# First product of three more regions in quarters, with the measures moved: a 4096-cubed matmul with leaky ReLU on one core

## The chip, the cores and the metric

The kernel runs on one core of a Trainium2 chip. A core has TensorE (PE) for matmuls, which write to PSUM, four engines beside it (VectorE, DVE; ScalarE, ACT; GpSimd, POOL; SyncE, SP), and 16 DMA engines that serve queues issued from SP, ACT and POOL. Every engine runs its instructions in order and waits on semaphores where it needs another engine's result. The metric is the device time of one execution in microseconds (us). The kernel before took 1514.64 us, the median of three runs (1513.80 to 1515.65).

## What is computed

```python
def setup_inputs():
    m, k, n = 4096, 4096, 4096
    return {"a": np.random.randn(m, k).astype(np.float32),
            "b": np.random.randn(k, n).astype(np.float32),
            "alpha": np.float32(0.01)}

def reference(a, b, alpha):
    x = np.matmul(a, b)
    return np.where(x > 0, x, alpha * x)
```

## The kernel before

**Tiling.** The output is cut into regions of 1024 x 1024, named (g, j): g is one of four groups of rows of A, j one of four pairs of column blocks of B. Region (0, 0) is computed first by its own code. Then one loop (`for i, (g, j) in enumerate(regions)`) goes over (0,1) (0,2) (0,3), then (1,2) (1,0) (1,3) (1,1), then (2,2) (2,0) (2,3) (2,1), then (3,2) (3,0) (3,1) (3,3). The inputs are rounded to 16 bits.

**Seven products.** A region is one step of Strassen's method in Winograd's form: A's group and B's pair are 2 x 2 blocks (of 512 x 2048 and 2048 x 512), and seven products of such blocks, numbered 0 to 6 in the code, make the region: a11 b11, a12 b21, s2 T2, s3 T3, s1 T1, a22 T4, s4 b22. The sums s1 to s4 of A are made once for a group; the sums of B are made in place in each region by VectorE (`b_sum`, L583): T3 = b22 - b12 in b12's tile, T2 = T3 + b11 in b11's tile, T4 = b21 - T2 in b21's, and T1 = b22 - T2 in b11's again. B's tiles come in two parts, k = 0 and 1 (in the later groups, part 1 first). A full product (`product`, L906) is 64 matmuls of 512 columns.

**Quarters.** Many products take a second step of the same method: seven quarter products (`quarter_product`, L750) of 16 matmuls of 256 columns, 112 half-width matmuls in place of what would be 128. They need sums of quarters of A's block and of B's block (called t(1) to t(4) for B), again from VectorE (L674 to L697), and copies or additions between banks. Group 0 has none of them in this loop. In most regions of the later groups products 3 to 6 are in quarters; in a region that turns to the next group (the last of its group, (1,1) and (2,1)) only product 3 is, in `fourth_in_quarters`, whose third quarter product uses t(4), made on L682 after t(2) on L680.

**The first product in quarters.** In the regions of the set `FIRST` (before: (2,0), (2,3), (3,0), (3,1), (3,3)) product 0 is in quarters too: `for_the_first` (L1126 to L1140) makes seven sums on VectorE during the seventh product of the region before, and `first_in_quarters` makes one more (L1157) and two additions in PSUM (L1164, L1166), with the copies L1153 to L1170 on ScalarE. The other full products of such a region run as 128 half-width matmuls (L887), since its banks hold quarters.

**Measures.** To judge at the end whether 16 bits were enough, the kernel sums squares of all blocks of A and B (`Measure`, L224 to L268): four squares by ScalarE (L233) into rooms of a 4 KB-per-partition tile, then additions, a fold and a reduction on VectorE (L242 to L267). `EARLY` lists which block a region measures ahead of or behind its T sums, `IN_C` the region that puts the squares in c's tiles. If the judgement fails, a slow path of plain matmuls runs instead; with this input it does not.

**Tiles and queues.** There are three tiles `a16` (rooms for squares, for quarters' sums and for pieces of the next group's A), two times two tiles `c0` and `c1` (results before they are stored; the regions take them in turn, `side`), three large tiles `x`, of which two hold s1 and s4 while the third is s2 in the first half of a region and the quarters' room after it, and two tiles for each of b11, b12, b21, b22. b's blocks come as 32-bit data through POOL's queue, which converts them (L541), or as 16-bit copies kept in DRAM (`kept`, `kept_half`, `kept_t`) through SP's queue (L536 to L538). SP also stores results (L1235) and loads s2 (L769) and kept sums. In a region that turns, which (0,3) does too, pieces of the next group's A come through POOL (L134) into `a16`, VectorE transposes them (L143) and ScalarE squares them (L600); a new piece is fetched when both have let go of an old one's tile.

**Order.** The program's order is written by hand and kept (`manual_schedule`): each engine executes its instructions in the order of the code. The steps that the prediction follows: in (0,3) T sums, transposes of four pieces, T4, four more, T1; in (1,1) and (2,1) a measure, the T sums, one transposed piece, a part of T4, t3 of b12, two pieces, a store's leaky ReLU, one piece, the other part of T4, t(2), t(4), t(1).

Of the kernel before, what the change touches and what calls it, by code (L numbers as in the profile page):

```python
# [36 lines left out]
LAST = 1  # L37
OTHERS = (0, 3)
KEPT_T = {CACHED: 1, 0: 2, 3: 2}

# [7 lines left out]
def kernel(  # L50
# [474 lines left out]
    def fetch_unit(i, u, nt, later=False):  # L525

        g, j = regions[i]
        half = u // 2
        t = b_pool.tile([P, KC, NT], DT, name="b", tag=f"b{half + 1}{nt + 1}")
        have_b[i, u, nt] = t  # L530
        if later:
            nc.vector.memset(t[:, :1, :1], 0.0)
        if g > KEPT_T.get(j, G) and (half, nt) == (0, 1):
            move_t("t3", j, t, u, False)
        elif g and j == CACHED:
            nc.sync.dma_start(t, rows_of(kept[nt], u, 0, KC, True))  # L536
        elif half and (g and j == LAST or g > 1 and j in OTHERS):
            nc.sync.dma_start(t.rearrange("p c n -> p (c n)"), kept_half[j][u - 2, nt])  # L538
        else:
            for c in range(0, KC, 4):  # L540
                nc.gpsimd.dma_start(t[:, c:c + 4, :], b_rows(j, u, c, 4, nt, g > 0))  # L541
            if j == CACHED:
                wide = KC // (RUNS + [1, 1])[u]
                for c in range(0, KC, wide):
                    nc.sync.dma_start(rows_of(kept[nt], u, c, wide, False), t[:, c:c + wide, :])
# [39 lines left out]
    def measure(i, which, x, y):  # L585

        if which:
            tiles = [have_b[i, 2 * x + k, y] for k in ((1, 0) if regions[i][0] else (0, 1))]
        else:
            tiles = [at[regions[i][0], x, 2 * y + k] for k in range(2)]  # L590
        parts = halves(tiles[0]) + halves(tiles[1])
        return Measure(which, parts, not which)
# [15 lines left out]
    def judge(line):  # L608
# [26 lines left out]
    A11, A12, A22 = (0, 0, 0), (0, 0, 1), (0, 1, 1)  # L635
    B11, B12, B21, B22 = ((1, half, nt) for half in range(2) for nt in range(2))
    EARLY = {
        (1, 0): [B21], (1, 3): [B11], (1, 1): [B11], (2, 3): [B21], (2, 1): [B12], (3, 1): [B21],
    }
    IN_C = (3, 0)  # L640
    MEASURED = {
        (0, 1): (None, [B22], B12, B11), (0, 2): (B21, [B22, A22, A11], B12, A12),
        (3, 3): (B22, [], None, None),
# [7 lines left out]
    kept_s2 = dram_pool.tile([2, P, KC * RM], DT, name="kept_s2")  # L651
    kept_q = {name: dram_pool.tile([4, P, QUARTER], DT, name=f"kept_q{name}") for name in ("a22", "s4", "s1")}
    made = dram_pool.tile([2, NT], DT, name="made")
    FIRST = {(2, 0), (2, 3), (3, 0), (3, 1), (3, 3)}
    kept_s3 = dram_pool.tile([P, QUARTER], DT, name="kept_s3")
    kept_x21 = {name: dram_pool.tile([P, QUARTER], DT, name=f"kept_x{name}") for name in ("a22", "s4")}
    side = 0
# [203 lines left out]
    for i, (g, j) in enumerate(regions):  # L861
# [10 lines left out]
        else:  # L872
            Y, Z = Z, Y

        def keep_half(some=(0, 1)):
            for nt in some:
                for k in ks:
                    nc.sync.dma_start(kept_half[j][k, nt], B(1, nt, k).rearrange("p c n -> p (c n)"))

        def product(n, banks, first):  # L880
# [401 lines left out]
        early = [measure(i, *block) for block in EARLY.get((g, j), [])]  # L1282
        have_t2 = g > KEPT_T.get(j, G)
        at_once, afterwards = ([], early) if in_first or have_t2 else (early[:1], early[1:])
        for m in at_once:
            m.begin()
        if first_of_group and g:
            keep_s2(g)
        if in_first:
            shared = new_bank(shared_bank)  # L1290
            first_in_quarters(y, shared, z, first_t, first_s)
            new_s(g, "s2")
            load_s2(g, ks[0])
        else:
            product(0, y, True)
        if second_of_group:
            sums_of_s3(g, (2,))
        for m in at_once:
# [4 lines left out]
        if have_t2:  # L1303
            for k in ks:
                t = have_b[i, k, 0] = b_pool.tile([P, KC, NT], DT, name="b", tag="b11")
                move_t("t2", j, t, k, False, nc.scalar)
        in_c = (g, j) == IN_C
        if in_c:
            m = measure(i, *B22)
            m.room = [c_pool.tile([P, 2048], BF16, name="sq", tag=f"c{n}") for n in (side, side, 1 - side, 1 - side)]  # L1310
            for n in range(4):
                m.square(n)
        if second_of_group:
            in_other = lambda n: c_pool.tile([P, QUARTER], DT, name="sums", tag=f"c{1 - side}") if n == 4 else new_a16()
            sums_of_a(g, "s1", in_other if g == 1 else new_a16, m.end if in_c else None)
# [19 lines left out]
            middle.end()  # L1335
        if i == 0:
            first_measure.end()
        for m in [] if have_t2 else afterwards:
            m.end()
        if final:  # L1340
            judged = judge(a16_pool.tile([1, P * 6], FP32, name="line", tag="a16"))
# [1 line left out]
        if (g, j) == (0, LAST):  # L1343
            for k in ks:
                nc.sync.dma_start(made[k:k + 1], B(0, 0, k)[:1, 0, :])
        if g == 1 and j in OTHERS or (g, j) == (0, LAST):
            keep_half((0,))
        note_rows()
        if first_of_group:
            sum_a(g, "s3")  # L1350
# [18 lines left out]
            b_sum(B(1, 0, ks[0]), B(1, 0, ks[0]), B(0, 0, ks[0]), SUB)  # L1369
        if final:  # L1370
            good = next(judged)
        if (g, j) == (0, LAST):
            keep_half((1,))
        for k in [] if in_fourth else ks[1:] if turning and g else ks:
            b_sum(B(1, 0, k), B(1, 0, k), B(0, 0, k), SUB)
# [15 lines left out]
        if in_fourth:  # L1391
            s5[3] = t[:, 3]
            load_sums("s1", s5, (3,))
            if g == 1 and j in OTHERS:
                keep_half((1,))
        if turning and g:
            tq, sx4 = {2: t[:, 0], 4: t[:, 1], 1: t[:, 2]}, t[:, 3]
            sums_of_b(quarters_of_b(i, 0, 1), tq, (2, 4, 1))
# [71 lines left out]
        elif turning and g:  # L1470
            v_pairs, v, parts = fourth_in_quarters(z, tq, {**s3_rooms(g), 4: a_quarter(sx4)})
            if turning:
                for n in range(3):
                    turn_a_in(0, 1, n)
            for n, (to, bank) in enumerate(parts):
                nc.vector.tensor_add(to, bank, to)
            if turning:
                add_v()
            if turning:
                z = [new_bank(Z[mt]) for mt in range(MT)]  # L1480
                for mt in range(MT):
                    nc.scalar.copy(z[mt], u2[mt])
        else:
            product(3, z, True)
            v_pairs, v = keep(z, side)
        if in_quarters and first_of_group:
            tq = {2: t[:, 0], 1: t[:, 1], 4: t[:, 2]}
        fetch_b(i + 1, [(0, 1)], (1, 0) if in_fourth else (0, 1) if turning and g else ks)
        if turning:
            new_s(g + 1, "s2")  # L1490
            if g:
                bring_a(0, 1, [3])
            note_rows(1)
            for n in range(3):
                fetch_a(1, 0, n)
            turn_a_in(1, 0, 0)
            fetch_a(1, 0, 3)
            load_x21(g, "a22")
            load_x21(g, "s4")
# [12 lines left out]
        if in_quarters:  # L1512
            banks = [new_bank(Z[n]) for n in range(MT)]
            tq, sq = sixth_in_quarters(u2_pairs, banks, v_pairs, v, y, tq, sq)
        else:
            add(v, y)
            leave(v_pairs, 1, 1)
        if turning:
            for n in range(1, MT):
# [9 lines left out]
        if not in_quarters:  # L1529
            product(5, z, False)  # L1530
            if g:
                for mt in range(MT):
                    nc.scalar.copy(u2[mt], z[mt])
            else:
                add(u2[::-1], z[::-1])
        if turning:
# [18 lines left out]
        if in_quarters:  # L1555
# [4 lines left out]
            if final:  # L1560
                even, last = seventh_at_the_end(*rest, new_bank(Z[1]), new_bank(Z[0]))
            else:
                first_t, first_s = {}, {}
                between = for_the_first(tq, sq, first_t, first_s) if next_first else nothing()
                kept_c = seventh_in_quarters(*rest, between)
                fetch_b(i + 1, [(1, 1)], (1, 0))
                if not next_first:
                    new_s(g, "s2")
                    load_s2(g, 1)
                leave(kept_c, 0, 1)  # L1570
# [83 lines left out]
```

## Time and profile before

| | |
|---|---|
| runs | 1514.64 us (median of 3) |
| profiled execution, its own time | 1514.02 us |
| span of the profile (first to last instruction) | 1512.2 us |
| TensorE busy | 1503.5 us, 99% of the span |
| VectorE busy | 1212.0 us, 80% |
| ScalarE busy | 527.7 us, 35% |
| DMA | 384.99 MB, 255 GB/s on the mean |
| region (0,3) | 312.31 to 409.00 us |
| region (1,3) | 592.87 to 683.37 us |
| region (1,1) | 683.37 to 778.47 us |
| region (2,1) | starts at 1050.39 us |

The profile is one execution, taken by the hardware profiler. Its span leaves out 1.8 us around the first and last instruction. In a row of the timeline stand start, length, engine, line of the code, operation, the tiles written and read, their shapes and the count of merged instructions; in brackets the idle time before it and what ended it. "SPq" and "ACTq" are issues of DMAs. The end of a matmul is modelled, so its drawn length overlaps the next one's start.

### The profile page before, as it was taken

To read this page: it belongs to the slowest core of one execution; us is meant where nothing else is said; L and a number is where in the kernel's file an instruction comes from. 1 tells how busy PE (TensorE), PEld (TensorE's weight loads), DVE (VectorE), ACT (ScalarE), POOL (GpSimd) and SP (SyncE) were. 2 spreads that over 40 slices of the span, in tenths; PEclk is the share of its full clock that TensorE was granted. 3 is DMA by queue.
4 is the path that set the end of the run, shared out by engine and by line. 5 is a ranking of instruction groups with operands and counts; after the bars stand their busy time and mean duration, and the time that the engine had idled before them with its cause. 6 is when DMAs were issued, how large, how long until landed. Compare 5 with 4: busy or idle time off the path is not lost.

```text
span 1512.2 us, 24641 instructions
## 1 busy us (share of the span) xinstructions
PE 1503.5 (99%) x9979; PEld 975.2 (64%) x9979; DVE 1212.0 (80%) x1259; ACT 527.7 (35%) x911; POOL 252.3 (17%) x418
## 2 busy tenths in 40 slices
PE   9999999999999999999999999999999999999998
PEld 4465444444446577584544788888554488888887
DVE  4599867786796797788779698987887878998797
ACT  2402535657410323126561122323574113242322
POOL 4641110233202011013220101000331000100000
PEclk9999999999999999999999999999999999999999
DMA  9999895999889999999898989979989697987845
GB/s 239 188 191 246 236 284 176 161 204 192 217 351 229 291 304 293 299 285 277 205 252 329 285 314 249 354 232 325 243 206 295 264 278 279 251 291 185 349 153 183
DMA packets 193970, 384.99 MB, mean 255 GB/s; under 512 B 17587, under 2 KB 126389, under 8 KB 178742
## 3 DMA queue, kind: packets, MB, share of 16 engines
q0 software_dynamic: 115584, 108.03, 45.0%
q1 hardware_dynamic: 71062, 245.53, 43.5%
q10 hardware_dynamic: 7200, 29.76, 5.0%
q8 instruction: 80, 1.31, 0.3%
q14 instruction: 44, 0.36, 0.1%
HBM read 359.66 MB, written 129.50 MB: 323 GB/s over the span
## 4 chain that ended last, share of the span: by engine, by line
PE 98%; DVE 1%; issue 0%; ACT 0%; DVEq 0%; ACTq 0%
PE ps L906 49%; PE ps L750 34%; PE ps L887 9%; PE ps L275 5%; PE wp L107 0%; DVE c L305 0%; DVE a L369 0%; DVE c L1188 0%; ACT a L369 0%; PE turned L362 0%; DVE q L1133 0%; DVE q L1132 0%; DVE q L1126 0%; DVE q L1137 0%; DVE a L733 0%
## 5 line engine op out<-in xcount | busy, mean ns | idle before, releaser
L906 PE MATMUL ps<-b,a 128*128 128x512 f16 x1984 | 431.6, 379 | 0.0
L906 PEld LDWEIGHTS <-a 128*128 128x128 f16 x1984 | 194.1, 98 | 233.0
L906 PE MATMUL ps<-b,s 128*128 128x512 f16 x1472 | 321.5, 379 | 0.0
L906 PEld LDWEIGHTS <-s 128*128 128x128 f16 x1472 | 144.0, 98 | 173.4 <-issue 0.2
L750 PEld LDWEIGHTS <-q 128*128 128x128 f16 x2192 | 214.1, 98 | 26.1 <-issue 0.7
L541 POOL DMA_DIRECT2D b<-in_b_dram x120 | 89.0, 746 | 848.2 <-PE ps L906 303.2
L583 DVE TENSOR_TENSOR b<-b 128x4096 f16<-128x4096 f16 x82 | 185.8, 2285 | 39.5 <-DMA b<-in_b_dram 30.4
L143 DVE STREAM_TRANSPOSE a<-a 128x512 uint32<-128x512 uint32 (+2 forms) x120 | 126.9, 1105 | 65.2 <-DMA a<-in_a_dram 65.2
L134 POOL DMA_DIRECT2D a<-in_a_dram x252 | 137.4, 553 | 249.8 <-ACT junk L600 82.2
L929 ACT COPY c<-ps 128x512 f32<-128x512 f32 x164 | 86.2, 595 | 262.8 <-PE ps L906 179.5
L750 PEld LDWEIGHTS <-a 128*128 128x128 f16 x1536 | 150.3, 98 | 18.7
L305 DVE SCALAR_TENSOR_TENSOR c<-c 128x1024 f32<-128x1024 f32 (+2 forms) x123 | 141.8, 1191 | 5.9 <-ACT c L929 5.6
L600 ACT ACTIVATE junk<-a 128x512 bf16<-128x512 f16 x192 | 121.2, 631 | 71.8 <-DMA a<-in_a_dram 49.8
L233 ACT ACTIVATE sq<-b 128x2048 bf16<-128x2048 f16 x60 | 111.4, 1910 | 62.9 <-DVE sq L242 54.7
L750 PE MATMUL ps<-b,q 128*128 128x256 f16 x1088 | 128.1, 273 | 0.0
L750 PE MATMUL ps<-q,q 128*128 128x256 f16 x1024 | 119.0, 273 | 0.0
L750 PE MATMUL ps<-b,a 128*128 128x256 f16 x976 | 114.5, 273 | 0.0
L750 PEld LDWEIGHTS <-s 128*128 128x128 f16 x960 | 93.9, 98 | 11.4
L275 PE MATMUL ps<-b,a 128*128 128x512 f16 x384 | 84.5, 379 | 1.8 <-DVE a L369 0.7
L887 PE MATMUL ps<-b,a 128*128 128x256 f16 x640 | 70.7, 273 | 0.0
L887 PE MATMUL ps<-b,s 128*128 128x256 f16 x640 | 70.7, 273 | 0.0
L934 DVE TENSOR_TENSOR c<-ps,c 128x512 f32<-128x512 f32 x76 | 47.0, 680 | 29.3 <-PE ps L906 29.3
(166 smaller groups left out, 1393.9 us busy)
## 6 DMA issues: line engine op xcount, KB each, us to landing
b<-in_b_dram POOLq DMA_DIRECT2D x128, 512.0 KB, 12.7
out_dram<-c SPq DMA_DIRECT2D x118, 512.0 KB, 8.2
a<-in_a_dram POOLq DMA_DIRECT2D x244, 128.0 KB, 5.6
b<-kept_half SPq DMA_DIRECT2D x28, 1024.0 KB, 11.9
b<-kept SPq DMA_DIRECT2D x20, 1024.0 KB, 9.4
q<-kept_qs ACTq DMA_DIRECT2D x40, 512.0 KB, 7.8
s<-kept_s SPq DMA_DIRECT2D x18, 1024.0 KB, 7.4
q<-kept_qs SPq DMA_DIRECT2D x28, 512.0 KB, 5.9
```

The costliest lines, as they stand in the source:

```text
L134: nc.gpsimd.dma_start(a16[32 * q:32 * q + 32], src.rearrange("(g i) w -> i g w", i=32))
L143: nc.vector.transpose(part.rearrange("p c m e -> p c (m e)").bitcast(U32) .rearrange("p c (g i) -> p g c i", i=32), src[:, :, i * n:(i + 1 ...
L233: nc.scalar.activation(to, self.parts[n], SQUARE)
L275: nc.tensor.matmul(ps, a_cols(at[0, h, u], c, mt), bt[0, u, nt][:, c, :], start=first, stop=last,)
L305: nc.vector.scalar_tensor_tensor(t, t, alpha, t, op0=MULT, op1=MAX if alpha <= 1 else MIN)
L541: nc.gpsimd.dma_start(t[:, c:c + 4, :], b_rows(j, u, c, 4, nt, g > 0))
L583: nc.vector.tensor_tensor(f(to), f(x0), f(x1), op)
L600: nc.scalar.activation(junk, piece[:, q, :], SQUARE, accum_out=to[:, 4 * n + q:4 * n + q + 1])
L750: nc.tensor.matmul(to[m], xq[:, c // 2, rows, c % 2], yq[:, c, :], start=first and c == 0 and m < banks, stop=c == KC - 1, skip_group_chec ...
L887: nc.tensor.matmul(to, a_cols(operand(g, name, k), c, q // 2 * 2 + m), B(half, nt, k)[:, c, q % 2 * HALF:(q % 2 + 1) * HALF], start=False, ...
L906: nc.tensor.matmul(banks[mt], a_cols(t, c, mt), B(half, nt, k)[:, c, :], start=first and (k, c) == todo[0], stop=(k, c) == todo[-1], skip_ ...
L929: nc.scalar.copy(to, bank)
```

## The change

- `FIRST` gains (1,3), (1,1) and (2,1): their product 0 is in quarters, their other full products in half-width matmuls. Lines that assumed whole banks now go by `pieces` (copies of z, of u2, and the addition of y).
- The measure of b11 in (1,3) goes to (0,3) (in both regions it is pair 3's b11), with its squares in c's tiles and one a16; it stays ahead of the T sums there. The measures of (1,1) (b11) and (2,1) (b12) put their four squares in c's tiles, behind the first product's copies, and their VectorE part comes behind the T sums.
- b22 of pair 3 is stored in 16 bits in (0,3) (`KEPT_IN`, `keep_half`), after b12 of the next region is fetched, and no longer in (1,3); (1,3) loads it from there on SP's queue. In place of standing behind the seventh product of (1,0), this load stands behind the first half of s2 in (1,3) (`LATE`).

Counted in the built program: SP issues 2 stores of 1 MB more in (0,3), 2 stores fewer and 2 loads more in (1,3), and POOL 4 loads of 512 KB fewer for (1,3). ScalarE's and VectorE's lists change only in the regions named.

```diff
--- before.py
+++ after.py
@@ -37,6 +37,8 @@
 LAST = 1
 OTHERS = (0, 3)
 KEPT_T = {CACHED: 1, 0: 2, 3: 2}
+KEPT_IN = {(LAST, 0): 0, (LAST, 1): 0, (0, 0): 1, (0, 1): 1, (3, 0): 1, (3, 1): 0}
+LATE = (1, 3)
 
 
 
@@ -534,7 +536,7 @@
             move_t("t3", j, t, u, False)
         elif g and j == CACHED:
             nc.sync.dma_start(t, rows_of(kept[nt], u, 0, KC, True))
-        elif half and (g and j == LAST or g > 1 and j in OTHERS):
+        elif half and g > KEPT_IN.get((j, nt), G):
             nc.sync.dma_start(t.rearrange("p c n -> p (c n)"), kept_half[j][u - 2, nt])
         else:
             for c in range(0, KC, 4):
@@ -635,9 +637,9 @@
     A11, A12, A22 = (0, 0, 0), (0, 0, 1), (0, 1, 1)
     B11, B12, B21, B22 = ((1, half, nt) for half in range(2) for nt in range(2))
     EARLY = {
-        (1, 0): [B21], (1, 3): [B11], (1, 1): [B11], (2, 3): [B21], (2, 1): [B12], (3, 1): [B21],
+        (0, 3): [B11], (1, 0): [B21], (2, 3): [B21], (3, 1): [B21],
     }
-    IN_C = (3, 0)
+    IN_C = {(1, 1): B11, (2, 1): B12, (3, 0): B22}
     MEASURED = {
         (0, 1): (None, [B22], B12, B11), (0, 2): (B21, [B22, A22, A11], B12, A12),
         (3, 3): (B22, [], None, None),
@@ -651,7 +653,7 @@
     kept_s2 = dram_pool.tile([2, P, KC * RM], DT, name="kept_s2")
     kept_q = {name: dram_pool.tile([4, P, QUARTER], DT, name=f"kept_q{name}") for name in ("a22", "s4", "s1")}
     made = dram_pool.tile([2, NT], DT, name="made")
-    FIRST = {(2, 0), (2, 3), (3, 0), (3, 1), (3, 3)}
+    FIRST = {LATE, (1, 1), (2, 0), (2, 3), (2, 1), (3, 0), (3, 1), (3, 3)}
     kept_s3 = dram_pool.tile([P, QUARTER], DT, name="kept_s3")
     kept_x21 = {name: dram_pool.tile([P, QUARTER], DT, name=f"kept_x{name}") for name in ("a22", "s4")}
     side = 0
@@ -872,9 +874,9 @@
         else:
             Y, Z = Z, Y
 
-        def keep_half(some=(0, 1)):
+        def keep_half(some):
             for nt in some:
-                for k in ks:
+                for k in ks if KEPT_IN.get((j, nt)) == g else ():
                     nc.sync.dma_start(kept_half[j][k, nt], B(1, nt, k).rearrange("p c n -> p (c n)"))
 
         def product(n, banks, first):
@@ -1282,6 +1284,9 @@
         early = [measure(i, *block) for block in EARLY.get((g, j), [])]
         have_t2 = g > KEPT_T.get(j, G)
         at_once, afterwards = ([], early) if in_first or have_t2 else (early[:1], early[1:])
+        if at_once and not g:
+            in_c = [c_pool.tile([P, 2048], BF16, name="sq", tag=f"c{side}") for _ in range(2)]
+            at_once[0].room = [*in_c, a16_pool.tile([P, 2048], BF16, name="sq", tag="a16"), in_c[1]]
         for m in at_once:
             m.begin()
         if first_of_group and g:
@@ -1293,6 +1298,8 @@
             load_s2(g, ks[0])
         else:
             product(0, y, True)
+        if (g, j) == LATE:
+            fetch_b(i, [(1, 1)], ks)
         if second_of_group:
             sums_of_s3(g, (2,))
         for m in at_once:
@@ -1304,12 +1311,15 @@
             for k in ks:
                 t = have_b[i, k, 0] = b_pool.tile([P, KC, NT], DT, name="b", tag="b11")
                 move_t("t2", j, t, k, False, nc.scalar)
-        in_c = (g, j) == IN_C
+        in_c = IN_C.get((g, j))
+        after_t2 = []
         if in_c:
-            m = measure(i, *B22)
+            m = measure(i, *in_c)
             m.room = [c_pool.tile([P, 2048], BF16, name="sq", tag=f"c{n}") for n in (side, side, 1 - side, 1 - side)]
             for n in range(4):
                 m.square(n)
+            if turning:
+                after_t2.append(m)
         if second_of_group:
             in_other = lambda n: c_pool.tile([P, QUARTER], DT, name="sums", tag=f"c{1 - side}") if n == 4 else new_a16()
             sums_of_a(g, "s1", in_other if g == 1 else new_a16, m.end if in_c else None)
@@ -1335,7 +1345,7 @@
             middle.end()
         if i == 0:
             first_measure.end()
-        for m in [] if have_t2 else afterwards:
+        for m in after_t2 if have_t2 else afterwards + after_t2:
             m.end()
         if final:
             judged = judge(a16_pool.tile([1, P * 6], FP32, name="line", tag="a16"))
@@ -1343,8 +1353,7 @@
         if (g, j) == (0, LAST):
             for k in ks:
                 nc.sync.dma_start(made[k:k + 1], B(0, 0, k)[:1, 0, :])
-        if g == 1 and j in OTHERS or (g, j) == (0, LAST):
-            keep_half((0,))
+        keep_half((0,))
         note_rows()
         if first_of_group:
             sum_a(g, "s3")
@@ -1369,7 +1378,7 @@
             b_sum(B(1, 0, ks[0]), B(1, 0, ks[0]), B(0, 0, ks[0]), SUB)
         if final:
             good = next(judged)
-        if (g, j) == (0, LAST):
+        if i == 0:
             keep_half((1,))
         for k in [] if in_fourth else ks[1:] if turning and g else ks:
             b_sum(B(1, 0, k), B(1, 0, k), B(0, 0, k), SUB)
@@ -1391,8 +1400,7 @@
         if in_fourth:
             s5[3] = t[:, 3]
             load_sums("s1", s5, (3,))
-            if g == 1 and j in OTHERS:
-                keep_half((1,))
+            keep_half((1,))
         if turning and g:
             tq, sx4 = {2: t[:, 0], 4: t[:, 1], 1: t[:, 2]}, t[:, 3]
             sums_of_b(quarters_of_b(i, 0, 1), tq, (2, 4, 1))
@@ -1478,14 +1486,16 @@
                 add_v()
             if turning:
                 z = [new_bank(Z[mt]) for mt in range(MT)]
-                for mt in range(MT):
-                    nc.scalar.copy(z[mt], u2[mt])
+                for to, bank in pieces(u2_pairs, z):
+                    nc.scalar.copy(bank, to)
         else:
             product(3, z, True)
             v_pairs, v = keep(z, side)
         if in_quarters and first_of_group:
             tq = {2: t[:, 0], 1: t[:, 1], 4: t[:, 2]}
         fetch_b(i + 1, [(0, 1)], (1, 0) if in_fourth else (0, 1) if turning and g else ks)
+        if not g and i:
+            keep_half((1,))
         if turning:
             new_s(g + 1, "s2")
             if g:
@@ -1513,7 +1523,7 @@
             banks = [new_bank(Z[n]) for n in range(MT)]
             tq, sq = sixth_in_quarters(u2_pairs, banks, v_pairs, v, y, tq, sq)
         else:
-            add(v, y)
+            add_pieces(v_pairs, y)
             leave(v_pairs, 1, 1)
         if turning:
             for n in range(1, MT):
@@ -1529,8 +1539,8 @@
         if not in_quarters:
             product(5, z, False)
             if g:
-                for mt in range(MT):
-                    nc.scalar.copy(u2[mt], z[mt])
+                for to, bank in pieces(u2_pairs, z):
+                    nc.scalar.copy(to, bank)
             else:
                 add(u2[::-1], z[::-1])
         if turning:
@@ -1563,7 +1573,8 @@
                 first_t, first_s = {}, {}
                 between = for_the_first(tq, sq, first_t, first_s) if next_first else nothing()
                 kept_c = seventh_in_quarters(*rest, between)
-                fetch_b(i + 1, [(1, 1)], (1, 0))
+                if regions[i + 1] != LATE:
+                    fetch_b(i + 1, [(1, 1)], (1, 0))
                 if not next_first:
                     new_s(g, "s2")
                     load_s2(g, 1)
```

## The prediction

> **What bounds the kernel now.** I read the page first (busy time, chain of waits), then what TensorE waited for, then the timelines of TensorE, VectorE, ScalarE and the issue queues around the changed regions. From the page:
>
> ```profile
> PE 1503.5 (99%) x9979; PEld 975.2 (64%) x9979; DVE 1212.0 (80%) x1259; ACT 527.7 (35%) x911; POOL 252.3 (17%) x418
> PE 98%; DVE 1%; issue 0%; ACT 0%; DVEq 0%; ACTq 0%
> ```
>
> Matmuls set the end. TensorE's longest wait after the first stage is this one, from the view of who waited for whom:
>
> ```profile
> PE ps L750 <- ACT ps L1153: 0.4, 1, 0.4
> ```
>
> So there is no stall to remove: a change gains only by shorter matmul work, and any lateness that it puts on VectorE, which is 80% busy, is paid in full once it is past that engine's slack. TensorE's timeline, in (0,3), then (1,3) and (1,1), then (2,3), which already starts in quarters (columns: start, length, group):
>
> ```profile
> 353.75 13.98 PE L906 MATMUL ps<-b,a 128*128 128x512 f16 x64
> 367.56 13.98 PE L906 MATMUL ps<-b,s 128*128 128x512 f16 x64
> ...
> 592.87 27.79 PE L906 MATMUL ps<-b,a 128*128 128x512 f16 x128
> 620.62 13.97 PE L906 MATMUL ps<-b,s 128*128 128x512 f16 x64
> ...
> 724.81 3.66 PE L750 MATMUL ps<-b,a 128*128 128x256 f16 x32
> 728.30 1.91 PE L750 MATMUL ps<-q,a 128*128 128x256 f16 x16
> ...
> 961.25 1.91 PE L750 MATMUL ps<-b,a 128*128 128x256 f16 x16
> 973.54 14.14 PE L887 MATMUL ps<-b,a 128*128 128x256 f16 x128
> 987.51 14.14 PE L887 MATMUL ps<-b,s 128*128 128x256 f16 x128
> ```
>
> Starts are what counts, since the drawn lengths overlap. A full product takes 367.56 - 353.75 = 13.81 us. The first product in quarters takes 973.54 - 961.25 = 12.29, its short wait for L1153 included. A product in half-width matmuls, which such a region uses for its other full products, takes 987.51 - 973.54 = 13.97.
>
> **The gain: TensorE's work.** Each of (1,3), (1,1), (2,1) saves 13.81 - 12.29 = 1.52 on its first product and pays 0.16 for each product that goes to half-width: products 1 and 2 in (1,3), products 1, 2, 4, 5 and 6 in the regions that turn to the next group, (1,1) and (2,1). That is -1.52 + 0.32 = -1.20, and twice -1.52 + 0.80 = -0.72: together **-2.64 us**. Everything else can only cost.
>
> **(1,1) and (2,1): VectorE reaches the fourth product late.** Let F be the start of a region's first product. The second product after it now starts at F + 12.29 + 13.97 = F + 26.26 and ends at F + 40.23; the fourth product's third quarter needs the sum t(4) at 728.30 - 724.81 = 3.49 after that, F + 43.72. Before, in (1,1), VectorE did this:
>
> ```profile
> 705.72 2.10 DVE L143 STREAM_TRANSPOSE a<-a 128x512 uint32<-128x512 uint32 x2
> ...
> 719.55 2.25 DVE L583 TENSOR_TENSOR b<-b 128x4096 f16<-128x4096 f16 x1
> 725.01 1.23 DVE L680 TENSOR_TENSOR q<-b 128x2048 f16<-128x2048 f16 x1 [3.21 <-PE ps L906]
> 726.27 1.23 DVE L682 TENSOR_TENSOR q<-b,q 128x2048 f16<-128x2048 f16 x1
> 727.41 1.22 DVE L684 TENSOR_TENSOR q<-b,q 128x2048 f16<-128x2048 f16 x1
> ```
>
> From the first transpose (705.72) to the last b21 sum (721.80) it works without a pause, 16.1 us, then idles 3.21 and makes t(2) and t(4) in 727.41 - 725.01 = 2.4: ready at 727.4, 0.9 before use. So the slack is 3.2 + 0.9. What comes ahead of that block now is read from (2,3), VectorE first, then ScalarE:
>
> ```profile
> 972.60 2.28 DVE L583 TENSOR_TENSOR b<-b 128x4096 f16<-128x4096 f16 x1
> 974.83 0.06 DVE L768 MEMSET s<- 128x1 f16 x1
> 974.91 6.82 DVE L583 TENSOR_TENSOR b<-b 128x4096 f16<-128x4096 f16 x3
> 981.65 1.22 DVE L242 TENSOR_TENSOR sq<-sq 128x2048 bf16<-128x2048 bf16 x1
> ...
> 984.85 1.22 DVE L246 TENSOR_TENSOR sq<-sq 128x2048 bf16<-128x2048 bf16 x1 [0.65 <-ACT sq L233]
> ...
> 988.82 2.35 DVE L305 SCALAR_TENSOR_TENSOR c<-c 128x1024 f32<-128x1024 f32 x2
> ...
> 974.27 5.51 ACT L233 ACTIVATE sq<-b 128x2048 bf16<-128x2048 f16 x3
> ```
>
> The T sums cannot start before F + 11.35 (972.60 - 961.25), since VectorE first serves the quarters. In (1,1) the measured block is B11, which T2 overwrites, so T2's first half waits for two squares. ScalarE starts them after its bank copies at F + 13.02 and spaces them 1.80: the second is done at F + 16.7, the fourth at F + 20.3. T2, T3, T2 then take 6.82: F + 23.6. The measure takes 988.82 - 981.65 less its wait, 6.5: F + 30.1. The block of 16.1 and the 2.4 follow: t(4) is there at F + 48.6, **4.9 us late**. In (2,1) the block is B12, which T3 overwrites, so all four T sums (9.1) stand behind F + 16.8: 2.3 later still, **7.2 us late**. Lower bound for both, if no square were waited for: T sums from F + 11.35, t(4) at F + 45.4, 1.7 late. Upper bound: 1 more, if a square waits for c's tile to be stored. Queued behind are T1, the transposes and the fourth product's additions; T1 is next, 4.5 us after t(1), and the fourth product's five remaining quarters cover it.
>
> **(0,3): the measure of (1,3)'s old place.** Its squares use c's two tiles that the region before has just stored. Issue and landing of those stores (the tile's view in that window):
>
> ```profile
> L1235 SPq DMA_DIRECT2D out_dram<-c x2: 372/372/373, 308.1 to 309.2; - x2
> DMA to landing us min/median/max: 8.9/9.6/10.3
> ```
>
> So the first square starts at 317.0 to 318.4, and the fourth, which reuses the second's tile, ends at 324.4 to 325.9. VectorE adds it in and folds in 988.82 - 984.85 = 4.0: 328.4 to 329.9. VectorE and the queue of A's fetches (POOL) before:
>
> ```profile
> 318.86 4.69 DVE L583 TENSOR_TENSOR b<-b 128x4096 f16<-128x4096 f16 x2
> 326.97 4.69 DVE L583 TENSOR_TENSOR b<-b 128x4096 f16<-128x4096 f16 x2 [3.42 <-DMA b<-in_b_dram]
> 331.58 6.08 DVE L143 STREAM_TRANSPOSE a<-a 128x512 uint32<-128x512 uint32 x6
> 341.07 2.11 DVE L143 STREAM_TRANSPOSE a<-a 128x512 uint32<-128x512 uint32 x2 [3.41 <-DMA a<-in_a_dram]
> ...
> 360.60 2.10 DVE L143 STREAM_TRANSPOSE a<-a 128x512 uint32<-128x512 uint32 x2 [2.84 <-DMA a<-in_a_dram]
> 362.62 4.45 DVE L583 TENSOR_TENSOR b<-b 128x4096 f16<-128x4096 f16 x2
> ...
> 334.23 4.31 POOL L134 DMA_DIRECT2D a<-in_a_dram  x8 [3.74 <-DVE a L143]
> ```
>
> The four T sums end 9.3 later, at 337.7 to 339.2 where it was 331.58: 6.1 to 7.6 late (T2 itself is in time for 339.94 in its first half). The waits of 3.41 and 2.84 do not absorb this: each is for a piece of A whose fetch waited for a buffer that an earlier transpose frees (the last row), so they move along. T1's first half was done at 364.8 for the product that starts at 367.56, 2.7 early: it is now **3.4 to 4.9 us late; I take 4.2**. TensorE might also wait 0.3 at 326.1 for ScalarE's copies behind the fourth square; lower bound of this part 2, if the fetches land sooner.
>
> **(1,3): b22 in 16 bits, behind s2.** Before, VectorE waited here and T2 was just in time for 620.62:
>
> ```profile
> 615.89 2.29 DVE L583 TENSOR_TENSOR b<-b 128x4096 f16<-128x4096 f16 x1 [9.76 <-DMA b<-in_b_dram]
> 618.27 2.29 DVE L583 TENSOR_TENSOR b<-b 128x4096 f16<-128x4096 f16 x1
> ```
>
> Now SP issues it after the first half of s2. How that queue ran in (2,3), with the landing of that region's b22:
>
> ```profile
> 971.98 3.29 SPq L769 DMA_DIRECT2D s<-kept_s  x2
> DMA to landing us min/median/max: 11.9/14.1/16.3
> ```
>
> s2 goes out at F + 10.7, b22 at F + 11.2. T3 and T2 take 4.6 and are needed at F + 26.26, so it has 10.4 us. At 11.9 TensorE waits 1.5, at 16.3 it waits 5.9, at 10 or less nothing. I take **1.5**. The 16-bit store of b22 in (0,3), two transfers of 1 MB on SP behind the loads of `kept`, has nothing urgent behind it before 384.63; the store of (1,3) that it replaces, and four POOL loads, fall away. (1,3) loses its measure, so its VectorE block is like that of (2,3), which did not stall. These cost nothing; if the stores delayed fetches of A, that would be in the range of (0,3).
>
> **Sum.** -2.64 + 4.9 + 7.2 + 4.2 + 1.5 = +15.2 on the profiled execution's 1514.02, 0.6 under the median: **1529 us**.
>
> **Rivals.**
> 1. *The clock falls after the stalls.* The kernel's first 11 matmuls show a cold start:
>
> ```profile
> 1.19 4.87 PE L107 MATMUL wp<-w 128*128 128x512 f16 x11 [1.19 <-DVE x L93]
> ```
>
> They took 443 ns each against 13.81 / 64 = 216, 2.5 us lost. If each of the three long stalls brings that back, the time is 1531.5 to 1537, say 1533. For it: the stalls of 4.9 and 7.2 would be the longest idle times of the run. Against it: no row shows TensorE idle in mid-run. The Trainium skill, "TensorE: Matmul & The Clock Gate", Part 1, says that an idle window of about 3.4 us halves the clock until a busy window has passed. By that rule 7.2 us always contains such a window and 4.9 us often, so one or two losses; no run here shows it yet.
> 2. *Less is late.* If VectorE's queue has the lower bounds everywhere (1.7, 1.7, 2, and no wait for b22), the sum is +2.8: 1517, and up to 1524 where half of it holds. Against it: the squares' start is tied to TensorE's own bank copies.
> 3. *It works: not slower.* The quarters' ten extra VectorE operations fall into idle time ahead of F, and the 3.2 + 0.9 of slack covers the rest: 1514.02 - 2.64 = 1511.4. It decides at t(4) before F + 43.7. For it: VectorE idles in such tails. Against it: the block of 16.1 + 2.4 is serial, and 31.8 us of work stand behind the squares.
> 4. *b22 comes as late as 16.3* and the rest as forecast: 1534.
>
> **How the numbers follow.** Chances: forecast 0.38, rival 1 0.22, rival 2 0.16, rival 3 0.15, rival 4 0.09. The range leaves out rival 3 and the top of 1: 1515 to 1536; the forecast's own range, from the terms' bounds, is 1524 to 1533. A measurement tells about 0.2%, 3.0 us, from no change. Rival 3 lies on that border: faster 0.08, same 0.07; rival 2 gives another 0.06 to same; slower 0.79.
>
> **What would show it.** First products of 12.3 us in the three regions, half-width ones of 13.97; TensorE idle some 5 and 7 us before the third quarter of the fourth product in (1,1) and (2,1), released by L682's line on VectorE; 4 us before product 4 of (0,3), released by a T1 sum; 1 to 2 before product 2 of (1,3). Wrong if TensorE is still 99% busy in a span near 1510, if t(4)'s operation ends before its quarter's turn, or if the clock row shows less than full speed there.

## The result, and the profile after

| | before | after |
|---|---|---|
| runs taken side by side, median | 1515.65 us (5 runs) | 1538.51 us (5 runs, 1536.01 to 1540.74) |
| ratio, 95% interval | | 1.0151 (1.0135 to 1.0167) |
| profiled execution, its own time | 1514.02 us | 1536.01 us |
| its span | 1512.2 us | 1534.2 us |

The change costs 1.5%. The forecast was 1529 us in a range of 1515 to 1536, so the median lies 2.5 us above the range. The profiled execution is the fastest of the five; its span is 22.0 us longer than before, and the rows below account for that. In the changed file the lines quoted of before stand a little lower: L583 is L585, L680 to L684 are L682 to L686, L750 is L752, L887 is L889, L906 is L908.

The page of after, busy time of the engines and the shares of the chain of waits:

```profile
PE 1508.3 (98%) x10891; PEld 1066.8 (70%) x10891; DVE 1243.8 (81%) x1285; ACT 534.4 (35%) x923; POOL 249.4 (16%) x414
PE 87%; DMA 6%; DVE 5%; issue 1%; ACT 0%; POOL 0%; DVEq 0%; SPq 0%; ACTq 0%
```

VectorE's share of the chain went from 1% to 5% and DMA has come in with 6%, although VectorE is only 81% busy. The view of who waited for whom says where (us in total, times, longest):

```profile
PE ps L752 <- DVE q L684: 11.1, 2, 6.6
PE ps L908 <- DVE b L585: 5.5, 1, 5.5
```

Three waits, where before had none over 0.4 us after the first stage: two for t(4) (the operation on L684) and one for a T sum. TensorE's timeline around them, in (0,3), (1,1) and (2,1):

```profile
354.73 13.98 PE L908 MATMUL ps<-b,a 128*128 128x512 f16 x64
374.24 16.16 PE L908 MATMUL ps<-b,s 128*128 128x512 f16 x64 [5.53 <-DVE b L585]
390.23 10.09 PE L908 MATMUL ps<-b,a 128*128 128x512 f16 x46
...
731.12 3.66 PE L752 MATMUL ps<-b,a 128*128 128x256 f16 x32
739.22 3.60 PE L752 MATMUL ps<-q,a 128*128 128x256 f16 x16 [4.44 <-DVE q L684]
742.61 2.55 PE L752 MATMUL ps<-q,s 128*128 128x256 f16 x16
744.99 1.91 PE L752 MATMUL ps<-q,a 128*128 128x256 f16 x16
...
1104.30 3.66 PE L752 MATMUL ps<-b,a 128*128 128x256 f16 x32
1114.59 3.60 PE L752 MATMUL ps<-q,a 128*128 128x256 f16 x16 [6.64 <-DVE q L684]
1117.98 2.59 PE L752 MATMUL ps<-q,s 128*128 128x256 f16 x16
1120.40 1.91 PE L752 MATMUL ps<-q,a 128*128 128x256 f16 x16
```

From start to start, with the full-speed durations of the prediction (13.81 for a product, 3.49 for two quarters): (0,3) is 374.24 - 354.73 - 13.81 = 5.70 late, (1,1) is 739.22 - 731.12 - 3.49 = 4.61 late, (2,1) is 1114.59 - 1104.30 - 3.49 = 6.80 late. That is 17.1 us. The work behind each wait is also slow: the product in (0,3) takes 15.99 where 13.81 is full speed, and the two quarters behind each t(4) take 3.39 and 2.38, or 3.39 and 2.42, where the one at 744.99 and those of before take 1.75. That is 2.18 + 2.27 + 2.31 = 6.8 us more. The granted clock in three stretches of 3.41 us, in the first of which the stall in (1,1) begins (columns: window, length, busy us of PE, PEld, DVE, ACT, POOL, then the granted clock, DMA share, GB/s):

```profile
733.65:737.07 3.42, 1.13 (x11) 0.77 (x8) 3.42 (x3) 1.04 (x3) 1.93 (x4) 1.00 0.95 205
737.07:740.48 3.41, 1.26 (x7) 0.89 (x8) 3.38 (x4) 0.58 (x1) 0.23 (x1) 0.50 1.14 294
740.48:743.89 3.41, 3.41 (x18) 2.41 (x17) 3.41 (x2) 0.59 (x1) 0.00 (x0) 0.50 1.15 270
```

TensorE ran at half its clock for two of these stretches, 6.8 us, and at full clock after them; the other two stalls are each followed by 6.8 us of half clock as well. So 17.1 of waits, 6.8 of matmul time lost to the half clock (the two figures of 6.8 agree by accident: the first is one spell's length, the second what three spells cost) and the gain of 2.64 make +21.2 of the 22.0. The rest is no more than the two executions differ by before the first changed region: (0,3) starts at 312.31 before and at 313.29 after.

### The profile page after: what moved, and what is told of

Read it like the earlier page. It is cut to its first block, busy times and chain, and to the rows that moved or that the text cites. A ratio compares the mean times of both kernels' runs of the same rounds, so it can differ in the third digit from the quotient of the medians.

```text
span 1534.2 us, 26503 instructions
## 1 busy us (share of the span) xinstructions
PE 1508.3 (98%) x10891; PEld 1066.8 (70%) x10891; DVE 1243.8 (81%) x1285; ACT 534.4 (35%) x923; POOL 249.4 (16%) x414
## 4 chain that ended last, share of the span: by engine, by line
PE 87%; DMA 6%; DVE 5%; issue 1%; ACT 0%; POOL 0%; DVEq 0%; SPq 0%; ACTq 0%
PE ps L752 34%; PE ps L908 32%; PE ps L889 16%; PE ps L277 5%; DMA b<-in_b_dram 3%; DVE b L585 2%; DMA a<-in_a_dram 2%; DVE a L145 1%; DMA out_dram<-c 1%; DVE c L307 1%; DMA a_in<-in_a_dram 0%; DVE sq L248 0%; DVE sq L244 0%; DVE a L371 0%; DVE sq L247 0%
## 5 line engine op out<-in xcount | busy, mean ns | idle before, releaser
L908 PE MATMUL ps<-b,a 128*128 128x512 f16 x1472 | 320.3, 379 | 0.3 <-DVE a L555 0.3
L908 PEld LDWEIGHTS <-a 128*128 128x128 f16 x1472 | 144.0, 98 | 173.3 <-DVE a L555 0.8
L752 PEld LDWEIGHTS <-q 128*128 128x128 f16 x2384 | 232.9, 98 | 28.1 <-issue 0.4
L908 PE MATMUL ps<-b,s 128*128 128x512 f16 x1024 | 225.8, 382 | 5.5 <-DVE b L585 5.5
L585 DVE TENSOR_TENSOR b<-b 128x4096 f16<-128x4096 f16 x82 | 185.6, 2286 | 47.4 <-DMA b<-in_b_dram 17.3
L908 PEld LDWEIGHTS <-s 128*128 128x128 f16 x1024 | 100.7, 98 | 128.2 <-DVE b L585 6.0
L752 PEld LDWEIGHTS <-a 128*128 128x128 f16 x1680 | 165.7, 99 | 32.9 <-DVE q L684 11.6
L889 PE MATMUL ps<-b,s 128*128 128x256 f16 x1536 | 169.6, 273 | 0.0
L889 PEld LDWEIGHTS <-s 128*128 128x128 f16 x1536 | 150.3, 98 | 17.4
L889 PE MATMUL ps<-b,a 128*128 128x256 f16 x1280 | 141.4, 273 | 0.0
L889 PEld LDWEIGHTS <-a 128*128 128x128 f16 x1280 | 125.2, 98 | 14.5
L752 PE MATMUL ps<-b,q 128*128 128x256 f16 x1136 | 133.8, 273 | 0.0
L752 PE MATMUL ps<-q,q 128*128 128x256 f16 x1120 | 130.4, 273 | 0.0
L752 PE MATMUL ps<-b,a 128*128 128x256 f16 x1072 | 126.0, 273 | 0.0
L752 PEld LDWEIGHTS <-s 128*128 128x128 f16 x960 | 94.7, 99 | 12.0
```

The lines of the kernel that those rows point to most:

```text
L585: nc.vector.tensor_tensor(f(to), f(x0), f(x1), op)
L752: nc.tensor.matmul(to[m], xq[:, c // 2, rows, c % 2], yq[:, c, :], start=first and c == 0 and m < banks, stop=c == KC - 1, skip_group_chec ...
L889: nc.tensor.matmul(to, a_cols(operand(g, name, k), c, q // 2 * 2 + m), B(half, nt, k)[:, c, q % 2 * HALF:(q % 2 + 1) * HALF], start=False, ...
L908: nc.tensor.matmul(banks[mt], a_cols(t, c, mt), B(half, nt, k)[:, c, :], start=first and (k, c) == todo[0], stop=(k, c) == todo[-1], skip_ ...
```

## The experiments

The edits are against the changed kernel. Each was timed beside the kernel before on the same chip, whose median was 1514.79 us for the first four and 1514.73 for the last four.

**1. No measure in (0,3).**

```diff
-        (0, 3): [B11], (1, 0): [B21], (2, 3): [B21], (3, 1): [B21],
+        (1, 0): [B21], (2, 3): [B21], (3, 1): [B21],
```

> The changed kernel without the measure of pair 3's b11 in (0,3): that sum of squares is left out. Theory (the measure delays the transposes and through them T1): TensorE's 5.7 us wait before product 4 of (0,3) is gone, and with it the half-speed clock that follows it (2.2 us): about 7.9 us less than the changed kernel, 1528 to 1531 us. Rival (the wait comes from the 16-bit store of b22 or from fetches of A that are slow for another reason): the wait stays, no change.

1529.02 us (4 runs, 1526.70 to 1532.67), ratio 1.0102 (1.0085 to 1.0119). The view of waits has lost the T sum's line and kept the other:

```profile
PE ps L752 <- DVE q L684: 11.1, 2, 6.7
```

The measure alone makes the stall in (0,3), and the waits in the regions that turn do not depend on it.

**2. No measure in (1,1) and (2,1).**

```diff
-    IN_C = {(1, 1): B11, (2, 1): B12, (3, 0): B22}
+    IN_C = {(3, 0): B22}
```

> The changed kernel without the measures of (1,1) and (2,1): their sums of squares are left out. Theory (measure plus the wait of T2 or T3 for its squares make t(4) late): VectorE's T sums start at F + 11.4, t(4) is there at about F + 39, ahead of F + 43.7; both waits (4.6 and 6.8 us) and both cold stretches (2.3 each) go: 16 us less than the changed kernel, 1520 to 1524 us. Rival (VectorE is late in any case because the first product's own sums fill it): waits of 2 us and more stay, 5 to 8 us less.

1519.49 us (6 runs, 1518.59 to 1521.68), ratio 1.0030 (1.0018 to 1.0043). That is 0.5 under the expected range. The mirror image in the same view, where L684 keeps 0.3:

```profile
PE ps L908 <- DVE b L585: 5.1, 1, 5.1
```

**3. Neither.** Both edits together.

> The changed kernel without the three measures of (0,3), (1,1) and (2,1): their sums of squares are left out. Theory: no stall of over 1 us is left and TensorE's shorter work shows alone: 2.6 us below the kernel before, about 1512 us, clock back to 1.000. Rival (another cost of the change was covered by the stalls, such as b22 behind s2 in (1,3)): a wait of 1.5 to 6 us appears in (1,3), 1514 to 1518 us.

1512.90 us (10 runs, 1511.34 to 1516.67), ratio 0.9991 (0.9982 to 1.0001), no mid-run wait over 0.9. All that the change loses stands on the three measures. It also shows the ceiling: with the time of these measures taken away altogether, quarters in three more first products are worth about 0.1%, which the interval does not tell from nothing.

**4. TensorE kept busy where it would stall.** Same work in front of t(4), but TensorE computes throw-away quarters (into a bank that is overwritten later), two in (1,1) and three in (2,1), before the one that needs it. In `fourth_in_quarters`, ahead of `x[1, 1], t(4)`:

```diff
+            for _ in range({(1, 1): 2, (2, 1): 3}.get((g, j), 0)):
+                quarter_product(x[0, 0], b[0, 0], into(other), True)
```

> The changed kernel with extra quarter products into a bank that is still unused, ahead of the third quarter of the fourth product: two in (1,1) (3.5 us of its 4.6 us wait), three in (2,1) (5.2 us of its 6.8). Their result is overwritten. Theory (the clock falls because TensorE idles over 3.4 us): what idle time is left is under 2 us, the clock stays full in both places, and 4.6 us (two times 2.3) are gained: 1531 to 1536 us. Rival (the slow matmuls after the wait have another cause, such as contention for SBUF with VectorE and DMA): the time stays that of the changed kernel.

1530.89 us (4 runs, 1530.10 to 1532.21), ratio 1.0104 (1.0088 to 1.0121), 7.6 under the changed kernel's median and 5.9 from fastest to fastest, although the two were not timed beside each other; the two profiled executions differ by 3.8, where 4.6 was expected. TensorE's timeline in (1,1):

```profile
731.63 7.15 PE L752 MATMUL ps<-b,a 128*128 128x256 f16 x64
739.74 1.92 PE L752 MATMUL ps<-q,a 128*128 128x256 f16 x16 [0.95 <-DVE q L684]
741.49 1.91 PE L752 MATMUL ps<-q,s 128*128 128x256 f16 x16
```

t(4) is as late as ever, 48.3 us after the start of the region in both, yet the quarter behind it takes 741.49 - 739.74 = 1.75 from start to start, full speed. The half clock comes from TensorE's idle time, not from what runs beside it, and more matmuls gave less time.

**5. The measured blocks exchanged.**

```diff
-    IN_C = {(1, 1): B11, (2, 1): B12, (3, 0): B22}
+    IN_C = {(1, 1): B12, (2, 1): B11, (3, 0): B22}
```

> The changed kernel with the two measured blocks exchanged: (1,1) measures b12, which T3 overwrites, and (2,1) measures b11, which T2 overwrites. My theory (what stands on VectorE between the second square and t(4) sets the stall): the four T sums wait for the second square in (1,1) now and only the last three in (2,1), so the stalls change places: about 6.8 us in (1,1) and 4.6 in (2,1), their sum 11.4 as before, the time that of the changed kernel, 1536 to 1541. Rival (the length belongs to the region, for instance to its transposes and fetches of A, or to the store of c's tile): 4.6 and 6.8 stay where they are.

One run, 1537.65 us. TensorE in (1,1) and (2,1):

```profile
730.02 3.66 PE L752 MATMUL ps<-b,a 128*128 128x256 f16 x32
740.53 3.59 PE L752 MATMUL ps<-q,a 128*128 128x256 f16 x16 [6.86 <-DVE q L684]
...
1105.75 3.66 PE L752 MATMUL ps<-b,a 128*128 128x256 f16 x32
1114.97 3.60 PE L752 MATMUL ps<-q,a 128*128 128x256 f16 x16 [5.56 <-DVE q L684]
```

From start to start the stalls are 740.53 - 730.02 - 3.49 = 7.02 in (1,1) and 1114.97 - 1105.75 - 3.49 = 5.73 in (2,1): they changed places. The second is 1.1 longer than the same block cost in (1,1). VectorE's timeline there shows why:

```profile
1082.29 4.49 DVE L585 TENSOR_TENSOR b<-b 128x4096 f16<-128x4096 f16 x2 [2.13 <-ACT sq L235]
1088.03 2.29 DVE L585 TENSOR_TENSOR b<-b 128x4096 f16<-128x4096 f16 x1 [1.25 <-ACT sq L235]
```

The last T sum waits 1.25 more for the fourth square. In (1,1) of the changed kernel the three ran on without such a gap.

**6. (1,3) alone.** (1,1) and (2,1) as before the change, no measure in (0,3); (1,3) in quarters measures its own b11, behind its T sums.

```diff
-        (0, 3): [B11], (1, 0): [B21], (2, 3): [B21], (3, 1): [B21],
+        (1, 0): [B21], (1, 1): [B11], (2, 3): [B21], (2, 1): [B12], (3, 1): [B21],
...
-    IN_C = {(1, 1): B11, (2, 1): B12, (3, 0): B22}
+    IN_C = {(1, 3): B11, (3, 0): B22}
...
-    FIRST = {LATE, (1, 1), (2, 0), (2, 3), (2, 1), (3, 0), (3, 1), (3, 3)}
+    FIRST = {LATE, (2, 0), (2, 3), (3, 0), (3, 1), (3, 3)}
...
-            if turning:
+            if not second_of_group:
                 after_t2.append(m)
```

> The changed kernel cut down to the part that has room: quarters in the first product of (1,3) alone, with its measure of b11 kept in (1,3), in c's tiles, behind the T sums; b22 in 16 bits as in the change; (1,1) and (2,1) as in the kernel before; no measure in (0,3). My theory: (1,3) does not turn to the next group, so it has none of the serial work ahead of t(2) and t(4); its T2 waits for the second square until F + 16.7 and ends at F + 23.6, ahead of F + 26.26. No stall over 0.9 us, full clock, and 1.2 us less than before: ratio 0.999, 1513 to 1516. Rival (any measure behind the first product's copies makes a late sum): a stall of 2 us or more in (1,3), 1517 or more.

1518.79 us (10 runs, 1516.13 to 1524.28), ratio 1.0026 (1.0015 to 1.0037): slower, and my theory missed. VectorE, then TensorE, in (1,3), whose F is 594.8 here:

```profile
615.04 2.29 DVE L585 TENSOR_TENSOR b<-b 128x4096 f16<-128x4096 f16 x1 [8.80 <-DMA b<-kept_half]
...
617.44 6.89 DVE L585 TENSOR_TENSOR b<-b 128x4096 f16<-128x4096 f16 x3
624.25 1.22 DVE L244 TENSOR_TENSOR sq<-sq 128x2048 bf16<-128x2048 bf16 x1
...
632.94 4.69 DVE L585 TENSOR_TENSOR b<-b 128x4096 f16<-128x4096 f16 x2
...
637.68 2.84 PE L752 MATMUL ps<-b,s 128*128 128x256 f16 x16 [2.48 <-DVE b L585]
641.08 2.30 PE L752 MATMUL ps<-b,s 128*128 128x256 f16 x16 [0.56 <-DVE b L1416]
643.22 1.91 PE L752 MATMUL ps<-b,q 128*128 128x256 f16 x16
```

I had the second square (F + 16.7) start the T sums. They started at F + 20.2, when b22 landed; VectorE stood idle for 8.8 before it. The measure behind them pushed the block at 632.94 past its use: waits of 2.48 and 0.56, and the quarters behind them slow (2.84 and 2.14 where 1.75 is full speed, 1.5 us together). The rival's 2 us or more was right.

**7. All three, everything measured, transposes moved behind t(1) and T1.** The measures as in the change for (1,1) and (2,1), as in 6 for (1,3).

```diff
-            bring_a(0, 0, [1, 2])
+            for n in (1, 2):
+                fetch_a(0, 0, n)
+                square_a(0, 0, n)
...
-        if g:
-            bring_a(0, 0, [3])
+        if turning and g:
+            fetch_a(0, 0, 3)
+            square_a(0, 0, 3)
...
-        if turning and g:
-            for n in range(3):
-                fetch_a(0, 1, n)
...
+        if turning and g:
+            for n in (1, 2, 3):
+                coming[0, 0][n][1]()
+            for n in range(3):
+                fetch_a(0, 1, n)
```

> All three regions in quarters and everything measured: (1,3) measures its b11 itself as in the run with (1,3) alone; in (1,1) and (2,1) the transposes of three pieces of A (6.15 us of VectorE) go behind t(1) and T1, so that t(2) and t(4) come that much earlier; the fetches of the next three pieces, which need the tiles that these transposes free, go behind them. My theory: t(4) at F + 42.1 in (1,1), no stall, and at F + 44.4 in (2,1), 0.7 late; no half clock. The next pieces come some 6 to 8 us later; VectorE waited 5.4 and 2.7 for such pieces later in these regions. If the later chain has that slack the time is 1512 to 1517. Rival (the lateness only moves on to the pieces of A): TensorE waits 3 to 8 us at or just after the start of (2,2) and (3,2), with a half clock after it, 1522 to 1535.

1547.25 us (4 runs, 1546.20 to 1547.41), ratio 1.0209 (1.0194 to 1.0225). The waits of TensorE:

```profile
PE ps L889 <- ACT ps L1495: 23.6, 2, 11.8
...
PE ps L752 <- DVE q L684: 0.7, 1, 0.7
```

The stall for t(4) is gone in (1,1) and 0.7 in (2,1), as worked out: VectorE's order did set it. The lateness came back as 11.8 in each of these two regions, larger than my rival's 3 to 8 and in the same region, not at the start of the next group, so the time is above both expected ranges. (1,3) waited too, 2.8 and 0.9 us, as in experiment 6. VectorE, then ScalarE, in (1,1):

```profile
738.14 6.10 DVE L145 STREAM_TRANSPOSE a<-a 128x512 uint32<-128x512 uint32 x6
752.06 2.12 DVE L145 STREAM_TRANSPOSE a<-a 128x512 uint32<-128x512 uint32 x2 [7.82 <-DMA a<-in_a_dram]
...
763.07 3.23 DVE L1489 TENSOR_TENSOR c<-ps,c 128x512 f32<-128x512 f32 x5
...
767.52 2.19 ACT L1495 COPY ps<-c 128x512 f32<-128x512 f32 x4 [3.49 <-DVE c L1230]
```

The next three pieces of A could be fetched only when the moved transposes let go of their tiles, so VectorE waited 7.82 for the first of them and again for the other two (3.02 and 1.78), and the fourth product's additions, which stand behind those transposes, were made from 763.07 where the changed kernel made them from 750.65. The bank copies for product 5 wait for the last of those additions.

**8. b22 of (1,3) in 32 bits again.** Experiment 3 with `(3, 1): 1` in `KEPT_IN`, `LATE = None` and `(1, 3)` written out in `FIRST`.

> The run with none of the three measures (their sums of squares are left out here too), but b22 of pair 3 comes to (1,3) as in the kernel before, in 32 bits through POOL's queue behind the seventh product of (1,0), and is stored in 16 bits in (1,3). There b22 had been the last to land, 23.0 us after the start of the region; T3 and T2 take 4.6 and product 2 now starts at F + 26.26. My theory: a wait of 1 to 1.5 us before product 2 of (1,3), so that the 16-bit copy of (0,3) is worth that; time 1511 to 1516. Rival (the copy was not needed, the fetch is early enough): no wait over 0.5 us there.

One run, 1512.64 us, and in the waits

```profile
PE ps L889 <- DVE b L585: 0.9, 1, 0.9
```

A wait of 0.9 before product 2 of (1,3), a little under my 1 to 1.5: in this one run b22's old fetch is late by that much once the first product is shorter. The times do not show that the 16-bit copy is worth more: 1512.64 here, a median of 1512.90 in experiment 3.

No version beats the kernel before by more than can be measured: 3 and 8, which leave the three sums of squares out, are the fastest.

## Why the prediction was too low

**What failed: the half clock after the stalls was left out of the sum, at nothing instead of 6.8 us.** The prediction made "the clock falls after the stalls" a rival with a chance of 0.22, beside a forecast with the same stalls at full clock, on the ground that "no row shows TensorE idle in mid-run". But the forecast itself had put three stalls of 4.2 to 7.2 us there; given those, the clock's fall was a consequence of the forecast, not another case. All three brought it, at 2.2 to 2.3 us each against the 2.5 of the rival. The rival's 1531.5 to 1537 was the forecast plus one to three such losses, and the range's upper end, 1536, cut off its top. Experiment 4 shows the cause: with idle time filled and t(4) unmoved, the full clock stays. The rule of the Trainium skill that the rival named ("TensorE: Matmul & The Clock Gate", Part 1) agrees with the fall, but its idle window, read as a stretch that is idle from end to end, was not needed. In (1,1) TensorE idled for 4.44 us, yet no whole stretch of 3.41 us was idle: the rows above have it busy for 1.13 and 1.26 in them.

The other steps:

- *The gain of 2.64* was right. In (1,3), the first product and the first half-width one:

```profile
601.72 1.91 PE L752 MATMUL ps<-b,a 128*128 128x256 f16 x16
...
614.00 14.14 PE L889 MATMUL ps<-b,a 128*128 128x256 f16 x128
627.98 14.14 PE L889 MATMUL ps<-b,s 128*128 128x256 f16 x128
```

  614.00 - 601.72 = 12.28 and 627.98 - 614.00 = 13.98, predicted 12.29 and 13.97.
- *(1,1) and (2,1)*, predicted 4.9 and 7.2: 4.61 and 6.80. VectorE in (1,1), whose F is 690.89:

```profile
707.65 6.89 DVE L585 TENSOR_TENSOR b<-b 128x4096 f16<-128x4096 f16 x3 [3.13 <-ACT sq L235]
714.46 1.22 DVE L244 TENSOR_TENSOR sq<-sq 128x2048 bf16<-128x2048 bf16 x1
...
720.88 2.12 DVE L145 STREAM_TRANSPOSE a<-a 128x512 uint32<-128x512 uint32 x2
...
737.94 1.23 DVE L684 TENSOR_TENSOR q<-b,q 128x2048 f16<-128x2048 f16 x1
```

  T2 waits for the second square until F + 16.76 (predicted F + 16.7), the measure takes 6.4 and t(4) is there 48.3 after F (predicted 48.6). Experiments 2, 5 and 7 show each part of this queue: the measure, which block is measured, and what stands between.
- *(0,3)*, predicted 4.2, was 5.70. VectorE there:

```profile
339.18 6.04 DVE L145 STREAM_TRANSPOSE a<-a 128x512 uint32<-128x512 uint32 x6
...
369.93 2.08 DVE L145 STREAM_TRANSPOSE a<-a 128x512 uint32<-128x512 uint32 x2 [4.98 <-DMA a<-in_a_dram]
371.92 4.46 DVE L585 TENSOR_TENSOR b<-b 128x4096 f16<-128x4096 f16 x2
```

  The T sums had ended when the transposes began, at 339.18. Counted from the start of the region (313.29 after, 312.31 before) that is 25.89 where it had been 19.27: 6.6 later, inside the forecast of 6.1 to 7.6. What was mis-sized is the last wait for a piece of A: 4.98 where it had been 2.84. I had said that these waits "move along"; this one grew by 2.1, past the bound of 4.9 us for the stall. The 16-bit store of b22 is not what held the piece up: SP issued it at 369.18, when the wait was all but over. Why that fetch was slower was not tried.
- *(1,3)*, predicted 1.5, was nothing. b22's issue and landing in (1,3):

```profile
L540 SPq DMA_DIRECT2D b<-kept_half x2: 431/440/448, 612.8 to 613.3; - x2
DMA to landing us min/median/max: 9.2/10.2/11.2
```

  It was issued at F + 11.1 as expected and landed in 9.2 to 11.2 us; the row of (2,3) that I priced it by had 11.9 to 16.3, for loads that went out at 954.5 and 961.4, ahead of that region and not behind s2. T3 and T2's first halves ended at about 626.8, 1.2 ahead of 627.98. Experiment 6 shows that there is little room behind them too: the 6.4 us of a measure behind those sums brought a wait of 2.48.
- *Rivals 2 and 3* fell with the serial block: no bound below the forecast held in the turns. *Rival 4* fell with the landing.

By the traces the sum is -2.64 + 4.61 + 6.80 + 5.70 + 6.8 = +21.2, where the prediction had +15.2. The median is 9.3 above the prediction's 1529.2: 6.0 of that is this difference, 1.6 is the kernel before, whose median beside it was 1515.65 and not the 1514.02 that the sum started from, and 1.6 is not traced. So without the half clock the median would have lain inside the range, and with it the profiled run, at 1536.01, lies on its edge.

What stays open is the spread: five runs of after cover 4.7 us, and the median is 2.5 above the profiled run. The half clock explains little of it: the mean granted clock of the two slowest runs is 0.993, as in the profiled one, and 0.001 of 1536 us is 1.5 us. Nor are stalls needed for such a spread, since the ten runs of experiment 3 cover 5.3 us without one. The records of one execution cannot say where the others lost it.

## What to carry to other kernels

A stall that a forecast puts on TensorE has a second price, which belongs in the same sum and not among the alternatives. Here it was 2.2 to 2.3 us for each of the three stalls of the changed kernel, and 1.5 to 2.9 over the experiments: in (0,3) alone, 1.7 behind the wait of 5.08 us in experiment 2, with one stretch at half clock, and 2.8 behind the 6.14 us in experiment 4, with two. Where an engine runs a hand-written order, find the operation with the nearest due time (t(4)) and add up all that stands ahead of it since the last thing it had to wait for; what is moved out of the way must be followed to its own deadline, as the transposes were here. And price the ceiling first: with the cost of the measures removed the idea was worth 0.1%, not told from nothing.

## What the hardware showed beyond that

The granted clock changed only at the borders of stretches of 3.41 us: its spells of half clock in mid-run lasted 3.41, 6.83, 10.24 or 13.65 us in all the traces, one to four such stretches. An idle time shorter than one stretch was enough to start one. In experiment 6, whose longest wait is 2.48 us, the stretches around it:

```profile
635.10:638.51 3.41, 0.93 (x9) 0.76 (x9) 3.31 (x3) 1.07 (x2) 0.00 (x0) 1.00 0.59 219
638.51:641.92 3.41, 2.85 (x15) 1.83 (x14) 3.41 (x4) 0.00 (x0) 0.00 (x0) 0.50 0.01 4
```

and in experiment 4, around the wait of 1.79 us in (2,1):

```profile
1110.27:1113.68 3.41, 1.62 (x16) 1.21 (x15) 3.38 (x4) 0.58 (x1) 1.09 (x2) 1.00 1.04 255
1113.68:1117.10 3.42, 3.42 (x34) 3.07 (x32) 3.42 (x3) 0.75 (x2) 0.00 (x0) 1.00 1.15 270
```

After a stretch in which TensorE was busy for 0.93 (or, in (1,1) of after, 1.13) of 3.41 us the clock halved; after one with 1.62 it did not. Stretch by stretch through all ten profiles no case stands against this, and the border is closer: the busiest stretch at full clock that was followed by half clock had 1.2 us (experiment 7, from 634.77), the least busy that was not had 1.5 (experiment 1, from 724.72). At half clock a stretch with up to 2.58 busy was followed by another at half clock (experiment 5, from 1114.13), one with 2.85, in the rows above, by full clock. These busy times rest on modelled ends of matmuls. The Trainium skill, "TensorE: Matmul & The Clock Gate", Part 1, gives an idle window of about 3.4 us as the condition; here about two thirds of one did it, and by this reading it depends on how a stall of 2 to 3 us lies to the borders whether it is caught. Experiment 1 shows the same for how long the clock stays down: its wait of 4.43 us in (1,1), as long as that of the changed kernel, fell into stretches with 1.5 and 0.9 busy, and only one stretch at half clock followed, 1.7 us lost.
